# A two-layer decoder trunk: q and k of the attention kept by halves of the sequence, the first pair's groups in that order, and scores ten steps ahead of the values

## The chip, the core and the metric

The kernel runs on one core of a Trainium2 chip. The core's engines have their own instruction queues and run side by side: TensorE (PE) multiplies matrices into PSUM, ScalarE (ACT) and VectorE (DVE) work on PSUM and SBUF, GpSimd (POOL) helps, and SyncE (SP) issues DMA transfers. An instruction that waits holds up everything behind it on its engine. The metric is the device time of one execution in microseconds (us), lower is better.

## The reference

One layer of a gated linear recurrence, one of stick-breaking attention, each followed by a SwiGLU feed-forward network (FFN), all in float32 on a sequence of 1024 tokens with width 1024. The attention, which the change touches, has 16 heads of 64:

```python
qkv = jnp.einsum("bsd,de->bse", x, w_qkv).reshape(bsz, seq, 3, N_HEADS, HEAD_DIM)
...
z = jnp.einsum("bhqd,bhkd->bhqk", qb, kb).astype(jnp.float32) * scale
...
log_fail = jnp.where(strict, jax.nn.log_sigmoid(-z), 0.0)
suffix = lax.cumsum(log_fail, axis=3, reverse=True) - log_fail
weights = jnp.where(strict, jnp.exp(jax.nn.log_sigmoid(z) + suffix), 0.0)
outs.append(jnp.einsum("bhqk,bhkd->bhqd", weights.astype(vb.dtype), vb))
```

Every query attends to earlier keys only; a key's weight is what the later keys left over of the stick.

## The kernel before

**Precision.** PE works on a rounded float32 (`F32R`). A full product is made of three matmuls, hi x hi, hi x lo and lo x hi (`mm3`, L140): each operand is split into a rounded part, copied by ACT, and the rest, subtracted by DVE.

**Pairs, groups and steps.** Heads go in eight pairs `q` of 128 columns. For each pair `qkv_steps(q)` (L1392) computes q, k and v (`which` 0, 1, 2), each for two halves `n` of the sequence (512 tokens). One of these six groups takes eight steps, one `mm3` each, so a pair has 48 steps. Before a `which` begins, the next weights are prepared: `next_weights` (L1377) hands three pieces to the list `later` (ACT copies, DVE subtractions), and `load_link` (L1370) issues on SP a load of weights further ahead.

**What follows a group.** `evacuate` (L1422) scales the product by the normalisation factor `rbc[n]` into `t` (DVE, L1436), and splits it into `two` (ACT L1444, DVE L1445). Four stores on SP then copy q or k into place: q needs hi and lo on different partitions (L1448, L1449), k is wanted twice, in the top and the bottom 64 partitions, for each head of the pair (L1452, `kk<-two`). All four read 64 partitions at a time. The tiles `Q[q][hx]` and `KK[q][hx]` cover all 1024 tokens; half `n` of the sequence fills its columns.

**Scores.** `chunk_list` cuts a head into twelve chunks: eight on the diagonal (row block j = 0..7, 128 to 512 columns of keys of the half j // 4), then four full ones (j = 4..7 against keys of the first half). A chunk is two matmuls on PE (`z_part`, L1481), a sigmoid on ACT and a running product on DVE (`z_rest`, L1493; scans at L1501 and L1504). Chunks 0 to 3 of a head read only the first halves of q and k; chunk 4 is the first that reads the second ones.

**Values.** A head has also twelve units (`unit_list`): `t_part` (L1510) transposes up to four blocks of weights on PE, ACT and DVE split them (`th`, `tl`), and `av_part` (L1530) multiplies them with v.

**The order written out by hand.** The loop at L1627 runs over units u from -LEAD (8) on. In each round PE gets, in this order: the scores of the next chunk, the transposes of unit u + 2, two fill steps (projections of later pairs, from `all_fill`), the values of unit u. ACT and DVE get `th`, `tl`, then the sigmoid and scan of the chunk, then one piece of `later`, then what the fill steps need. So chunk c stands in round c - 8; three extra chunks, in the rounds `gains` (L1621) 31, 29 and 27 from the end, raise the lead to eleven for the last rounds. Pair q's steps fall in the rounds before unit 24q: its first half of k is through in round 24q - 14, its second in 24q - 10.

**The prelude.** Before that loop, 34 steps of pair 0 run alone (L1614): q's two groups, k's two, two steps of v. The normalisation factors aren't known at the start; the dictionary `between` (L1606) places their sums (`stats`), their broadcasts and q's two waiting evacuations between the steps. q's two groups hold their products in the PSUM tiles of the scores (`psZ`), the others use `psQ`.

Of the kernel before, what the change touches and what calls it, by code (L numbers as in the profile page):

```python
# [8 lines left out]
F32 = mybir.dt.float32  # L9
F32R = mybir.dt.float32r  # L10
# [6 lines left out]
P = 128  # L17
S = 1024
D = 1024
ND = D // P  # L20
NT = S // P
NB = 512
NH = S // NB
# [10 lines left out]
def trunk(  # L34
# [22 lines left out]
    nc = tc.nc  # L57
    f32 = lambda t: t.bitcast(F32)
# [40 lines left out]
    xh, xl = [None] * ND, [None] * ND  # L99
# [1230 lines left out]
    NP = HEADS // 2  # L1330
# [12 lines left out]
    with ExitStack() as st:  # L1343
# [33 lines left out]
        def next_weights(raw, lo_eng=nc.vector):  # L1377
            hi, lo = wtile("whi"), wtile("wlo")
            part_hi = lambda i: nc.scalar.copy(half(hi, i), half(raw, i))
            part_lo = lambda i: lo_eng.tensor_sub(half(lo, i), half(raw, i), f32(half(hi, i)))  # L1380

            def second():
                part_lo(0)
                part_hi(1)

            later.extend((lambda: part_hi(0), second, lambda: part_lo(1)))
            k3 = lambda t: t.rearrange("p (k c) -> p k c", k=ND)
            return k3(hi), k3(lo)
# [1 line left out]


        def qkv_steps(q):  # L1392
            for which in range(3):
                w, at = wq.pop((q, which)), 3 * q + which + 1
                if at < 3 * NP:
                    wq[divmod(at, 3)] = next_weights(raws.pop(at))
                else:
                    mix[0].w[mix[0].order[0]] = next_weights(mix[0].raw.pop(0))
                for i in (at + 1,) if at < 3 * NP else (at + 1, at + 2):
                    load_link(i)  # L1400

                ks = (1, 5, 2, 6, 3, 7, 0, 4) if (q, which) == (0, 0) else range(ND)
                for n in range(NH):
                    pool, tag = (psZ, "z") if (q, which) == (0, 0) else (psQ, "qk")
                    ps = pool.tile([P, NB], F32, tag=tag, name="qk_ps")
                    for i, k in enumerate(ks):
                        mm3(ps, w[0][:, k], w[1][:, k], xh[k][n], xl[k][n], i == 0, i == ND - 1)
                        if i == 5 and late:
                            late.pop()()
                        if i < ND - 1:  # L1410
                            yield
                    ev = evacuate(q, which, n, ps)
                    if (q, which) == (0, 0):
                        waiting.append(ev)
                        yield
                    else:
                        next(ev)
                        yield
                        next(ev, None)


        def evacuate(q, which, n, ps):  # L1422
            full = lambda tag, m: [ap.tile([P, m, S], F32R, tag=tag, name=tag, bufs=4) for _ in range(2)]
            t = ap.tile([P, NB], F32, tag="t", name="t", bufs=2)
            cs = slice(n * NB, (n + 1) * NB)
            if which == 2:

                if n == 0:
                    VT[q] = ap.tile([P, S + 1], F32, tag="vt", name="vt", bufs=2)
                    nc.gpsimd.memset(VT[q][:, 0:1], 0.0)  # L1430
                after = VT[q][:, n * NB + 1 : (n + 1) * NB + 1]
                nc.vector.tensor_mul(after, ps, rbc[n])
                yield
                nc.vector.tensor_sub(t, VT[q][:, cs], after)
            else:
                nc.vector.tensor_mul(t, ps, rbc[n])  # L1436
                yield
            if which == 0 and n == 0:
                Q[q] = [t[:, 0] for t in full("q", 1)]
            if which == 1 and n == 0:  # L1440
                KK[q] = full("kk", 2)
            if which < 2:
                two = ap.tile([P, 2, NB], F32R, tag="two", name="two", bufs=2)
                nc.scalar.copy(two[:, 0], t)  # L1444
                nc.vector.tensor_sub(two[:, 1], t, f32(two)[:, 0])  # L1445
                for hx, (a, b) in enumerate(((top, bot), (bot, top))):
                    if which == 0:
                        nc.sync.dma_start(f32(Q[q][hx])[a, cs], f32(two)[a, 0])  # L1448
                        nc.sync.dma_start(f32(Q[q][hx])[b, cs], f32(two)[a, 1])  # L1449
                    else:  # L1450
                        for half_ in (top, bot):
                            nc.sync.dma_start(f32(KK[q][hx])[half_, :, cs], f32(two)[a])  # L1452
                return
            if n == 0:
                VV[q] = ap.tile([P, NT, 2, P], F32R, tag="v", name="v", bufs=2)

            def v_turn():

                pool, tag = (psT, "T") if (q, n) == (NP - 1, 1) else (psQ, "qk")
                tp = pool.tile([P, NB], F32, tag=tag, name="vt_ps")  # L1460
                for i in range(4):
                    nc.tensor.transpose(tp[:, i * P : (i + 1) * P], t[:, i * P : (i + 1) * P], ident)
                src = tp.rearrange("p (b h c) -> p b h c", b=4, h=2)
                bs = slice(4 * n, 4 * n + 4)
                vh, vl = (VV[q][:, bs, :, c] for c in (slice(0, HD), slice(HD, P)))
                nc.scalar.copy(vh, src)
                nc.vector.tensor_sub(vl, src, f32(vh))

            late.append(v_turn)
            if q == NP - 1 and n == 0:  # L1470
                bring_back(*((p, 0) for p in range(NP - 2)))
# [9 lines left out]
        def z_part(q, hx, j, ci, c0, c1, diag):  # L1481
            nk = (j + 1) * P
            ps = psZ.tile([P, NB], F32, tag="z", name="z_ps")
            lhsT = Q[q][hx][:, j * P : (j + 1) * P]
            nc.tensor.matmul(ps[:, 0 : c1 - c0], lhsT=lhsT, rhs=KK[q][hx][:, 0, c0:c1], start=True, stop=False)  # L1485
            nc.tensor.matmul(ps[:, 0 : c1 - c0], lhsT=lhsT, rhs=KK[q][hx][:, 1, c0:c1], start=False, stop=True)  # L1486
            return ps


# [79 lines left out]
        heads = [(q, hx) for q in range(NP) for hx in range(2)]  # L1569
        chunks = [c for q, hx in heads for c in chunk_list(q, hx)]  # L1570
        units = [u for q, hx in heads for u in unit_list(q, hx)]
        LEAD = 8

        def all_fill():
            yield from first
# [25 lines left out]
        with tc.manual_schedule(engines={E.PE, E.Activation, E.DVE, E.Pool, E.SP}):  # L1601


            load_link(1)
            first = qkv_steps(0)
            between = {  # L1606
                12: lambda: stats(rbc[0], psO, "o", 0),
                16: lambda: stats(rbc[1], psO, "o", 1),
                17: lambda: broadcast_r(psO, "o", 0),
                18: lambda: [*waiting[0]],  # L1610
                21: lambda: broadcast_r(psO, "o", 1),
                22: lambda: [*waiting[1]],
            }
            for i in range(1, 2 * ND * NH + 3):  # L1614
                next(first)
                if i in between:
                    between[i]()
                if i > 4 and later:
                    later.pop(0)()

            gains = [len(units) - x for x in (31, 29, 27)]  # L1621

            last_two, out_work = len(units) - 2 * 12, out_fill()
            amount = {x: 2 for x in (-1, 0, 1, 9, 10, 11, 12)}
            amount.update({x: 1 for x in range(14, 21)})
            c = 0
            for u in range(-LEAD, len(units)):  # L1627
                some = chunks[c : c + 1]
                c += 1
                for a in some:  # L1630
                    z = z_part(*a)
                if 0 <= u + 2 < len(units):
                    ready[u + 2] = t_split(t_part(*units[u + 2]), *units[u + 2])
                for a in some:
                    z_rest(z, *a)
                if u - last_two == 1:
                    late.pop()()
                if u - last_two == 9:
                    mix[0].w[mix[0].order[1]] = next_weights(mix[0].raw.pop(1), nc.gpsimd)
                if later:  # L1640
                    later.pop(0)()
                for _ in range(2):
                    next(fill, None)
                for _ in range(amount.get(u - last_two, 0)):
                    next(out_work)
                if u in gains:
                    z_rest(z_part(*chunks[c]), *chunks[c])
                    c += 1
                if u >= 0:
                    av_part(ready.pop(u), *units[u])  # L1650
            while later:
                later.pop(0)()
# [48 lines left out]
```

## Time and profile before

| what | us |
|---|---|
| median of three runs | 2182.03 (2181.58 to 2183.69) |
| the profiled execution | 2182.58 |
| its span, first to last instruction | 2180.8 |
| PE busy in the span | 2165.1 |
| first projection of the attention / first scores / last scores of the last pair start | 956.4 / 986.4 / 1442 |

The profile is of one execution. Busy times are unions of an engine's instructions. Matmul ends are modelled and overlap the next start: two matmuls of 512 columns follow each other every 0.23 us though each is shown with 0.39. In the timeline a row has start, duration, engine, line, operation and tiles, and in brackets the idle time before it with what ended it; in the chain of waits a row has start, duration and what; rows of the waits view have the total, the number of times and the longest; rows of stretches have each engine's busy time with its number of instructions, the granted clock, the DMA share and GB/s. `q` behind an engine's name marks its instruction queue, which issues DMAs.

### The profile page before, as it was taken

What the parts mean: (1) busy time and instruction counts of PE and PEld (TensorE: products, weight loads), DVE (VectorE), ACT (ScalarE), POOL (GpSimd) and SP (SyncE); (2) the same over time, 40 slices, a digit from 0 to 9 for tenths busy, and PEclk for the clock granted to TensorE, in tenths of its full rate; (3) what the DMA queues carried; (4) which work ended last, traced back from release to release, by engine and by line L of the source; (5) the groups of instructions that cost most, each with busy time, mean ns of one, the idle gap of its engine ahead of it and who ended that gap; (6) DMA issues with size and microseconds to landing.
All of it is one profiled execution on the core that took longest, in us unless ns stands there. A gap on an engine that the chain in (4) does not pass through costs nothing.

```text
span 2180.8 us, 27420 instructions
## 1 busy us (share of the span) xinstructions
PE 2165.1 (99%) x10122; PEld 1801.2 (83%) x10122; DVE 1703.7 (78%) x2381; ACT 1077.0 (49%) x1765; POOL 112.2 (5%) x84
## 2 busy tenths in 40 slices
PE   8999999999999999999999999999999999999998
PEld 7888888888888888888888888888888888888887
DVE  7888777767777887887888888886877777788886
ACT  6667445334444544554555555553534444454556
POOL 1222020000000000000000000002000000000002
PEclk9999999999999999999999999999999999999999
DMA  7111412334444764434333344551133444467452
GB/s 233 49 49 39 135 39 73 102 126 157 138 146 139 248 222 129 146 120 101 98 97 93 94 105 107 149 194 55 57 115 119 146 144 149 141 231 233 136 154 87
DMA packets 296101, 277.64 MB, mean 127 GB/s; under 512 B 15256, under 2 KB 210976, under 8 KB 295968
## 3 DMA queue, kind: packets, MB, share of 16 engines
q1 hardware_dynamic: 295808, 275.64, 40.7%
q8 instruction: 79, 1.29, 0.2%
q14 instruction: 54, 0.44, 0.1%
q10 hardware_dynamic: 160, 0.27, 0.0%
HBM read 175.71 MB, written 74.97 MB: 115 GB/s over the span
## 4 chain that ended last, share of the span: by engine, by line
PE 96%; DVE 2%; ACT 1%; DMA 0%; issue 0%; DVEq 0%; SPq 0%; ACTq 0%
PE p_ps L143 18%; PE p_ps L141 18%; PE p_ps L142 18%; PE qk_ps L141 4%; PE qk_ps L143 4%; PE qk_ps L142 4%; PE wt_ps L1515 3%; PE a_ps L142 3%; PE a_ps L143 3%; PE a_ps L141 3%; PE ob_ps L141 3%; PE ob_ps L142 2%; PE ob_ps L143 2%; PE z_ps L1485 2%; PE z_ps L1486 2%; PE av_ps L1537 2%
## 5 line engine op out<-in xcount | busy, mean ns | idle before, releaser
L143 PE MATMUL p_ps<-vh,wbl 128*128 128x512 f32 x524 | 204.2, 390 | 0.2 <-DVE wbl L716 0.2
L143 PE MATMUL p_ps<-vh,wal 128*128 128x512 f32 x524 | 204.1, 389 | 0.1
L141 PE MATMUL p_ps<-vh,wch 128*128 128x512 f32 x524 | 204.2, 390 | 0.0
L141 PE MATMUL p_ps<-vh,wbh 128*128 128x512 f32 x524 | 204.2, 390 | 0.0
L143 PE MATMUL p_ps<-vh,wcl 128*128 128x512 f32 x524 | 204.1, 390 | 0.0
L142 PE MATMUL p_ps<-vl,wbh 128*128 128x512 f32 x524 | 203.9, 389 | 0.0
L141 PE MATMUL p_ps<-vh,wah 128*128 128x512 f32 x524 | 203.9, 389 | 0.0
L142 PE MATMUL p_ps<-vl,wch 128*128 128x512 f32 x524 | 203.9, 389 | 0.0
L142 PE MATMUL p_ps<-vl,wah 128*128 128x512 f32 x524 | 203.8, 389 | 0.0
L1524 ACT CAST th<-wt_ps 128x512 fp32r<-128x512 f32 x192 | 92.1, 480 | 209.6 <-PE wt_ps L1515 209.4
L712 ACT CAST wbh<-sb 128x1024 fp32r<-128x1024 f32 (+2 forms) x69 | 69.6, 1009 | 194.2 <-DVE sb L696 194.2
L1525 DVE TENSOR_TENSOR tl<-wt_ps,th 128x512 fp32r<-128x512 f32 x192 | 106.0, 552 | 62.9 <-ACT th L1524 61.1
L141 PE MATMUL qk_ps<-vh,whi 128*128 128x512 f32 x264 | 118.3, 448 | 0.0
L143 PEld LDWEIGHTS p_ps<-vh,wbl 128*128 128x128 f32 x524 | 98.3, 188 | 22.0 <-DVE wbl L716 1.5
L143 PEld LDWEIGHTS p_ps<-vh,wal 128*128 128x128 f32 x524 | 98.4, 188 | 21.4 <-DVE wal L707 1.0
L143 PEld LDWEIGHTS p_ps<-vh,wcl 128*128 128x128 f32 x524 | 98.3, 188 | 21.2 <-DVE wcl L726 0.7
L142 PEld LDWEIGHTS p_ps<-vl,wah 128*128 128x128 f32 x524 | 98.3, 188 | 20.5
L141 PEld LDWEIGHTS p_ps<-vh,wch 128*128 128x128 f32 x524 | 98.4, 188 | 20.4 <-ACT tb L1103 0.2
L142 PEld LDWEIGHTS p_ps<-vl,wch 128*128 128x128 f32 x524 | 98.4, 188 | 20.4
L142 PEld LDWEIGHTS p_ps<-vl,wbh 128*128 128x128 f32 x524 | 98.4, 188 | 20.4
L141 PEld LDWEIGHTS p_ps<-vh,wbh 128*128 128x128 f32 x524 | 98.4, 188 | 20.3 <-ACT ta L1103 0.2
L141 PEld LDWEIGHTS p_ps<-vh,wah 128*128 128x128 f32 x524 | 98.3, 188 | 20.3
(353 smaller groups left out, 5566.1 us busy)
## 6 DMA issues: line engine op xcount, KB each, us to landing
raw<-in_ffn_w_in SPq DMA_DIRECT2D x88, 512.0 KB, 3.9
vl<-pd SPq DMA_DIRECT2D x128, 256.0 KB, 3.5
pd<-U SPq DMA_DIRECT2D x90, 256.0 KB, 2.3
kk<-two SPq DMA_DIRECT2D x64, 256.0 KB, 3.9
raw<-in_ffn_w_out SPq DMA_DIRECT2D x56, 256.0 KB, 3.7
raw<-in_attn_w_qkv SPq DMA_DIRECT2D x24, 512.0 KB, 4.1
q<-two SPq DMA_DIRECT2D x64, 128.0 KB, 2.3
raw<-in_lru_w_in SPq DMA_DIRECT2D x15, 512.0 KB, 3.9
```

Source lines behind the costliest of these rows:

```text
L141: nc.tensor.matmul(ps, lhsT=wh, rhs=mh, start=first, stop=False, **kw)
L142: nc.tensor.matmul(ps, lhsT=wh, rhs=ml, start=False, stop=False, **kw)
L143: nc.tensor.matmul(ps, lhsT=wl, rhs=mh, start=False, stop=last, **kw)
L712: nc.scalar.copy(self.full(self.wb), self.full(self.sb))
L1485: nc.tensor.matmul(ps[:, 0 : c1 - c0], lhsT=lhsT, rhs=KK[q][hx][:, 0, c0:c1], start=True, stop=False)
L1486: nc.tensor.matmul(ps[:, 0 : c1 - c0], lhsT=lhsT, rhs=KK[q][hx][:, 1, c0:c1], start=False, stop=True)
L1515: nc.tensor.transpose(tp[:, c : c + P], W[q, hx, j, kb // 4][:, (kb % 4) * P : (kb % 4 + 1) * P], ident)
L1524: nc.scalar.copy(th[:, q0:], tp[:, q0:])
L1525: nc.vector.tensor_sub(tl[:, q0:], tp[:, q0:], f32(th)[:, q0:])
L1537: nc.tensor.matmul(ps[:, q0:], lhsT=VV[q][:, kb, hx], rhs=tl[:, q0:], start=False, stop=last)
```

## The change

1. `Q` and `KK` are kept by halves: a tile for each pair, half and head (`Q[q, n][hx]`, `KK[q, n][hx]`) of 512 tokens, eight buffers of half the size in place of four. A store of k now writes rows of two times 512 numbers that lie in one piece. `z_part` picks the half.
2. For pair 0 alone the groups run q half 0, k half 0, q half 1, k half 1, then v. The two first ones wait in `psZ` for their factor; the second evacuation moves from place 22 to 19, ahead of the second broadcast. The next weights and the load ahead come with k's second half for pair 0 (for all other groups with the first half, as before).
3. LEAD is 10. The prelude has 30 steps, `later` is served from step 4 on, and of the three extra chunks only the first is left, so the lead is again eleven from there on.

```diff
         def qkv_steps(q):
-            for which in range(3):
-                w, at = wq.pop((q, which)), 3 * q + which + 1
-                if at < 3 * NP:
-                    wq[divmod(at, 3)] = next_weights(raws.pop(at))
...
+            groups = [(which, n) for which in range(3) for n in range(NH)]
+            if q == 0:
+
+                groups[1:3] = groups[2:0:-1]
+            w = {}
+            for which, n in groups:
+                if which not in w:
+                    w[which] = wq.pop((q, which))
+
+                if n == ((q, which) == (0, 1)):
+                    at = 3 * q + which + 1
+                    if at < 3 * NP:
+                        wq[divmod(at, 3)] = next_weights(raws.pop(at))
...
+                    for i in (at + 1,) if at < 3 * NP else (at + 1, at + 2):
+                        load_link(i)
+                early = q == n == 0 and which < 2
...
+                pool, tag = (psZ, "z") if early else (psQ, "qk")
...
         def evacuate(q, which, n, ps):
-            full = lambda tag, m: [ap.tile([P, m, S], F32R, tag=tag, name=tag, bufs=4) for _ in range(2)]
+            halves = lambda tag, m: [ap.tile([P, m, NB], F32R, tag=tag, name=tag, bufs=8) for _ in range(2)]
...
-            if which == 0 and n == 0:
-                Q[q] = [t[:, 0] for t in full("q", 1)]
-            if which == 1 and n == 0:
-                KK[q] = full("kk", 2)
+            if which == 0:
+                Q[q, n] = [t[:, 0] for t in halves("q", 1)]
+            if which == 1:
+                KK[q, n] = halves("kk", 2)
...
                         for half_ in (top, bot):
-                            nc.sync.dma_start(f32(KK[q][hx])[half_, :, cs], f32(two)[a])
+                            nc.sync.dma_start(f32(KK[q, n][hx])[half_], f32(two)[a])
...
-            lhsT = Q[q][hx][:, j * P : (j + 1) * P]
-            nc.tensor.matmul(ps[:, 0 : c1 - c0], lhsT=lhsT, rhs=KK[q][hx][:, 0, c0:c1], start=True, stop=False)
-            nc.tensor.matmul(ps[:, 0 : c1 - c0], lhsT=lhsT, rhs=KK[q][hx][:, 1, c0:c1], start=False, stop=True)
+            lhsT = Q[q, j // 4][hx][:, j % 4 * P : (j % 4 + 1) * P]
+            for i in range(2):
+                nc.tensor.matmul(
+                    ps[:, 0 : c1 - c0], lhsT=lhsT, rhs=KK[q, ci][hx][:, i, 0 : c1 - c0], start=i == 0, stop=i == 1
+                )
...
-        LEAD = 8
+        LEAD = 10
...
                 18: lambda: [*waiting[0]],
+                19: lambda: [*waiting[1]],
                 21: lambda: broadcast_r(psO, "o", 1),
-                22: lambda: [*waiting[1]],
             }
-            for i in range(1, 2 * ND * NH + 3):
+            for i in range(1, 2 * ND * NH - 1):
                 next(first)
                 if i in between:
                     between[i]()
-                if i > 4 and later:
+                if i > 3 and later:
                     later.pop(0)()
 
-            gains = [len(units) - x for x in (31, 29, 27)]
+            gains = [len(units) - 31]
```

More of the change, by code (lines that the diff above doesn't have):

```diff
@@ L1392, in qkv_steps @@
         def qkv_steps(q):
-            for which in range(3):
-                w, at = wq.pop((q, which)), 3 * q + which + 1
-                if at < 3 * NP:
-                    wq[divmod(at, 3)] = next_weights(raws.pop(at))
-                else:
[L1398 to L1419, printed above, removed]
@@ new lines, in qkv_steps @@
+            groups = [(which, n) for which in range(3) for n in range(NH)]
[9 more added lines that the diff above has]
+                        wq[divmod(at, 3)] = next_weights(raws.pop(at))
+                    else:
+                        mix[0].w[mix[0].order[0]] = next_weights(mix[0].raw.pop(0))
+                    for i in (at + 1,) if at < 3 * NP else (at + 1, at + 2):
+                        load_link(i)
+                early = q == n == 0 and which < 2
+                ks = (1, 5, 2, 6, 3, 7, 0, 4) if (q, which) == (0, 0) else range(ND)
+                pool, tag = (psZ, "z") if early else (psQ, "qk")
+                ps = pool.tile([P, NB], F32, tag=tag, name="qk_ps")
+                wh, wl = w[which]
+                for i, k in enumerate(ks):
+                    mm3(ps, wh[:, k], wl[:, k], xh[k][n], xl[k][n], i == 0, i == ND - 1)
+                    if i == 5 and late:
+                        late.pop()()
+                    if i < ND - 1:
+                        yield
+                ev = evacuate(q, which, n, ps)
+                if early:
+                    waiting.append(ev)
+                    yield
+                else:
+                    next(ev)
+                    yield
+                    next(ev, None)
@@ L1447, in evacuate @@
                     if which == 0:
-                        nc.sync.dma_start(f32(Q[q][hx])[a, cs], f32(two)[a, 0])
-                        nc.sync.dma_start(f32(Q[q][hx])[b, cs], f32(two)[a, 1])
+                        nc.sync.dma_start(f32(Q[q, n][hx])[a], f32(two)[a, 0])
+                        nc.sync.dma_start(f32(Q[q, n][hx])[b], f32(two)[a, 1])
                     else:
                         for half_ in (top, bot):
-                            nc.sync.dma_start(f32(KK[q][hx])[half_, :, cs], f32(two)[a])
+                            nc.sync.dma_start(f32(KK[q, n][hx])[half_], f32(two)[a])
                 return
```

## The prediction

> **What bounds the kernel now.** I read the page first, then the waits of TensorE (PE) in the attention stretch, a table of stretches, and the timeline of one pair of heads engine by engine.
>
> ```profile
> span 2180.8 us, 27420 instructions
> PE 2165.1 (99%) x10122; PEld 1801.2 (83%) x10122; DVE 1703.7 (78%) x2381; ACT 1077.0 (49%) x1765; POOL 112.2 (5%) x84
> ```
> ```profile
> PE wt_ps L1515 <- DVE tl L1525: 1.2, 3, 0.7
> PE z_ps L1485 <- DMA kk<-two: 1.1, 1, 1.1
> ...
> 1183.00:1243.00 60.00, 60.00 (x324) 50.80 (x323) 51.08 (x76) 30.64 (x66) 2.29 (x3) 1.00 0.37 97
> ```
>
> PE is busy 99% of the span. Between 985 and 1470 us only two things hold it: one wait of 1.1 us for the copies of K, and 1.2 us at the very end of attention, where the lead is eleven chunks before and after. A steady stretch (1183 to 1243) has PE busy 60.00 of 60. So ten steps of lead can win at most about 1.1 us, and whatever PE newly waits for is added to the time whole. The question is what the shorter distance to the score matmuls does.
>
> **The one wait that can go (pair 0).** The chain of waits:
>
> ```profile
> 973.54 0.70 DVE t L1436
> ...
> 974.97 0.69 DVE two L1445
> ...
> 979.48 0.70 DVE t L1436
> ...
> 981.62 0.65 SPq L1452
> ...
> 982.31 3.96 DMA kk<-two
> 986.27 0.14 issue
> 986.40 0.35 PE z_ps L1485
> ```
>
> A head's first score matmul needs two of a K half's four stores; they leave SyncE (SP) 0.69 apart, the second lands 3.96 after its issue, and PE goes 0.14 later. Scaling (t) to first store is 2.14 us (979.48 to 981.62). With K's first half computed second, its t can follow q's split, at 974.97 + 0.69 = 975.66, and its first store leaves at 977.80, 3.8 us earlier; the matmul could go at 982.6. The prelude is four steps shorter. Two steps take 1.37 us (1.81 from the transposes at 1215.36 below to the values at 1217.17, less four transposes):
>
> ```profile
> 997.43 0.44 PE wt_ps L1515 x4
> ```
>
> So PE arrives four steps, 2.7 us, sooner. It was ready at about 985.15 (the last projection matmul started at 984.92, and they follow each other every 0.23); now at 982.4. The old loss of 1.25 shrinks to about 0.1: **gain 1.15**.
>
> The moved work issues the same DMAs, in another order: K's first four stores pass q's second four on SP, and the loads of v's and the next q's weights come eight steps later. The split of v's weights then runs on ScalarE (ACT) and VectorE (DVE) behind q's second half (K's first split done at 977.8, then a copy of r, t, copy and subtraction of 0.7 each, and two lo halves of 0.6: 981.8); its first user, step 33, is at about 984.5. K's weights are needed eight steps sooner, at 963.76; their lo halves were written at 961.03 and 962.89 (0.68 each), the second needed only four steps into the group. Both at nothing; without that cover each costs the few tenths by which it is late.
>
> **What comes due two rounds earlier in every pair.** Fill steps keep their place against the transposes and values (34 steps before round -8, as before), so K of pair p is still ready in the same rounds; but chunk 24p is asked for in round 24p-10, not 24p-8, and chunk 24p+4, the first to read K's second half, in 24p-6, not 24p-4. Pair 4, rounds 82 to 90, on PE and SP:
>
> ```profile
> 1206.96 0.39 PE L1536 MATMUL av_ps<-th,v 128*128 128x512 f32 x1
> ...
> 1214.90 0.39 PE L1485 MATMUL z_ps<-kk,q 128*128 128x512 f32 x1
> ...
> 1215.36 0.60 PE L1515 MATMUL wt_ps<-ident,w 128*128 128x128 f32 x4
> ...
> 1217.17 0.28 PE L1536 MATMUL av_ps<-th,v 128*128 128x256 f32 x1
> ...
> 1222.12 0.28 PE L1485 MATMUL z_ps<-kk,q 128*128 128x256 f32 x1
> ...
> 1222.36 0.27 PE L1515 MATMUL wt_ps<-ident,w 128*128 128x128 f32 x1
> ...
> 1224.20 0.34 PE L1485 MATMUL z_ps<-kk,q 128*128 128x384 f32 x1
> ```
> ```profile
> 1211.33 13.29 SPq L1452 DMA_DIRECT2D kk<-two  x8
> ```
>
> K's first half is through PE at 1206.96 (the values follow the fill); its first store leaves at +4.37. Round 86 asks for scores at 1214.90, +7.94: the place chunk 96 moves to. Already in this trace 1211.33 + 0.69 + 3.96 is 1215.98, later than that.
>
> VectorE's order decides the delay:
>
> ```profile
> 1206.99 0.94 DVE L1501 TENSOR_TENSOR_SCAN w<-w,unit 128x384 f32<-128x384 f32 x1
> 1207.85 0.66 DVE L1380 TENSOR_TENSOR wlo<-raw,whi 128x512 fp32r<-128x512 f32 x1
> 1208.44 0.68 DVE L1436 TENSOR_TENSOR t<-qk_ps,rbc 128x512 f32<-128x512 f32 x1
> ...
> 1209.50 1.21 DVE L1501 TENSOR_TENSOR_SCAN w<-w,unit 128x512 f32<-128x512 f32 x1
> 1210.63 0.67 DVE L1445 TENSOR_TENSOR two<-t,two 128x512 fp32r<-128x512 f32 x1
> ...
> 1211.90 1.28 DVE L1504 TENSOR_TENSOR_SCAN w<-w,w 128x512 f32<-128x512 f32 x1
> ```
>
> Both t and the split's subtraction stand behind a round's scan. Two chunks further on, rounds 82 and 83 scan the previous head's full chunks (1.28 each, in place of 0.94 and 1.21): first store at 4.37 + 0.34 + 0.07 = +4.78.
>
> The new transfer has rows of 4 KB in place of 2 KB on both sides; the trace has none like it. Nearest rows:
>
> ```profile
> L1452 SPq DMA_DIRECT2D kk<-two x64: 590/660/1335, 981.6 to 1402.3; - x64
> ...
> DMA to landing us min/median/max: 3.0/3.9/5.4
> ...
> L1449 SPq DMA_DIRECT2D q<-two x32: 461/541/600, 975.7 to 1381.6; - x32
> ...
> pd<-U SPq DMA_DIRECT2D x90, 256.0 KB, 2.3
> ```
>
> I take 0.54 for the first issue (q's stores have the same 64 rows a store) and 3.9 to landing (same source, same 64 partitions, same bytes). Ends: 0.69 for the issue; 2.3 to landing, the row of equal size that runs from all 128 partitions. Beside this, the Trainium skill ("SBUF — State Buffer", section "Door 1: The DMA port swizzle") says partitions 0 to 63 reach only half of the ports and measures 196 GB/s there; an estimate from that is 2.7 us for the two stores' 512 KB whatever the row length, so by that rule the 2.3 end is out and the sum stands; by the other row it would be a gain.
>
> First half: 4.78 + 0.54 + 3.9 + 0.14 = 9.36 against 7.94: **PE waits 1.42**.
>
> Second half, through PE at 1217.17, asked for at 1224.20, +7.03. The rows that delayed it, and those of the narrow chunks that now stand there:
>
> ```profile
> 1217.22 1.28 DVE L1504 TENSOR_TENSOR_SCAN w<-w,w 128x512 f32<-128x512 f32 x1
> 1218.41 0.67 DVE L1436 TENSOR_TENSOR t<-qk_ps,rbc 128x512 f32<-128x512 f32 x1
> ...
> 1220.65 0.67 DVE L1445 TENSOR_TENSOR two<-t,two 128x512 fp32r<-128x512 f32 x1
> ...
> 1221.57 0.42 DVE L1501 TENSOR_TENSOR_SCAN w<-w,unit 128x128 f32<-128x128 f32 x1
> ```
> ```profile
> 1204.41 0.68 DVE L1501 TENSOR_TENSOR_SCAN w<-w,unit 128x256 f32<-128x256 f32 x1
> ```
> ```profile
> 1218.40 0.48 ACT L1524 CAST th<-wt_ps 128x384 fp32r<-128x384 f32 x1 [1.32 <-PE wt_ps L1515]
> 1218.77 0.61 ACT L1498 ACTIVATE w<-z_ps 128x512 f32<-128x512 f32 x1
> 1219.26 0.62 ACT L1444 CAST two<-t 128x512 fp32r<-128x512 f32 x1
> ...
> 1222.88 0.39 ACT L1498 ACTIVATE w<-z_ps 128x256 f32<-128x256 f32 x1
> ```
>
> Now chunk 96 (scan 0.42) and 97 (0.68) are in front: t at +0.47 in place of +1.24. On ACT the copy of th comes 0.22 sooner (scores of 256 columns take 0.24, not 0.46), at +1.01, its sigmoid ends at +1.77, the split's copy at +2.32; DVE scans until +2.48, subtracts until +3.15, first store at +3.2. Landed and seen: 3.2 + 0.54 + 3.9 + 0.14 = 7.78. The scores between change by -0.22, +0.11 and +0.22, so PE arrives at 7.14: **waits 0.64**. Behind the waiting matmul stand the round's transposes and fill, so everything is later by that much.
>
> **Sum.** Pairs 1 to 7: 7 x (1.42 + 0.64) = 14.4. In pair 7 round 161's extra chunk is chunk 172, the first to read K's second half, ahead of that round's values: 0.35 more. Pair 0's second half: PE is at chunk 4 three rounds after chunk 1, at 989.3; K is through at 984.1, its first store leaves at 986.4, seen at 991.0: 1.7. Less the gain: 14.4 + 0.35 + 1.7 - 1.15 = 15.3. The profiled execution took 2182.58 (2180.8 of span and 1.8 around it, untouched), 0.55 above the shown median: 2182.58 + 15.3, **2198 us**.
>
> **Rivals.** (1) *Only the first halves wait*: if the second half's store leaves 0.64 sooner still, 15.3 - 4.5 - 0.35 gives 2193. For it: ACT's and DVE's idle gaps there; against: I already took all of the scan's shortening. (2) *Not slower*: the stores of 4 KB rows land like the 2.3 row, 1.6 sooner. From 1.42 sooner on, no wait of pairs 1 to 7 is left, and pair 0 keeps 0.1: 2182.58 - 1.05 = 2181.5. For it: half the rows per store; against: the minimum of K's 64 stores is 3.0. (3) *The wait is for all four stores of a half*: two more issues of 0.54 and a landing nearer the 5.4 maximum, about 1.9 on each of 15 waits: 2226. Against: in pair 0 the matmul went 0.14 behind the second landing. (4) That the lead isn't ten on PE is excluded by PE keeping the written order in the timeline.
>
> **How the numbers follow.** Forecast 0.66, with a range of its own of 2193 to 2204 (0.15 more for the issue and 0.3 in VectorE's order, on 15 waits); rival 1 0.13; rival 2 0.12; rival 3 0.04; something at the seam to the FFN, either way, 0.05. The range 2188 to 2208 takes in the forecast and rival 1. A measurement here tells about 0.2%, 4.4 us, from no change: rival 2 falls within it. Faster 0.04, same 0.11, slower 0.85.
>
> **What would show it.** PE's waits list the score matmul behind K's stores some 15 times, about 15 to 17 us in all, two per pair, the longer at the chunk that reads K's first half; pair 0's first scores near 982.5; DVE and ACT busy time unchanged; PE no longer 60 of 60. Wrong: stores landing under 3 us, waits of a second kind, or time lost before 980 us.

## The result and the profile after

| | us |
|---|---|
| before, median of six runs beside the changed kernel | 2183.2 (2181.58 to 2183.85) |
| after, median of six runs | 2200.02 (2198.07 to 2200.99) |
| ratio after / before, 95% interval | 1.0078 (1.0068 to 1.0088) |
| the profiled executions, before and after | 2182.58 and 2198.07 |
| their spans | 2180.8 and 2196.3 |

The change makes the kernel slower by 0.8%, or 15.5 us between the two profiled executions. The forecast was 2198.0. That it meets the profiled 2198.07 so closely is in part luck: this execution is the fastest of the six, and the medians lie 16.8 us apart where the forecast had 15.3.

The page of the changed kernel, each engine's busy time, with its share of the span and its number of instructions.

```profile
PE 2167.8 (99%) x10122; PEld 1799.3 (82%) x10122; DVE 1707.2 (78%) x2381; ACT 1077.8 (49%) x1765; POOL 112.4 (5%) x84
```

PE has the same 10122 matmuls and is busy 2.7 us more, DVE 3.5 us more, ACT 0.8 us: the work is the same. The time went into PE standing still. PE's waits in the attention stretch of the changed kernel (970 to 1490 us; total, times, longest):

```profile
PE z_ps L1496 <- DMA kk<-two: 9.5, 11, 1.5
PE z_ps L1496 <- issue: 4.3, 3, 1.6
PE wt_ps L1527 <- DVE tl L1537: 1.2, 3, 0.7
PE z_ps L1496 <- ACT whi L1379: 0.8, 1, 0.8
```

Three of these rows are one thing. They hold 11 + 3 + 1 = 15 waits of a score matmul, 14.6 us in all; wherever the trace has the landing, the wait ends 0.14 us after the second store of a K half has landed, also where the view, which puts a wait down to whatever happened to end last, says "issue" or names a weights copy. Only the 1.2 us at the end of attention stand as before. The steady stretch, in which PE was busy 60.00 of 60 us, shows the same loss:

```profile
1183.00:1243.00 60.00, 58.21 (x310) 48.84 (x310) 49.21 (x73) 29.82 (x65) 2.28 (x3) 1.00 0.36 93
```

The missing 1.79 us are the two waits of pair 4. They stand in the timeline of PE (start, duration, tile sizes; in brackets the idle time before the row):

```profile
1213.78 0.39 PE L1548 MATMUL av_ps<-th,v 128*128 128x512 f32 x1
...
1221.52 0.34 PE L1549 MATMUL av_ps<-tl,v 128*128 128x384 f32 x1
1223.09 0.47 PE L1496 MATMUL z_ps<-kk,q 128*128 128x256 f32 x2 [1.23 <-DMA kk<-two]
...
1225.23 0.28 PE L1548 MATMUL av_ps<-th,v 128*128 128x256 f32 x1
1225.35 0.28 PE L1549 MATMUL av_ps<-tl,v 128*128 128x256 f32 x1
1225.46 0.41 PE L1496 MATMUL z_ps<-kk,q 128*128 128x256 f32 x2
...
1233.08 0.48 PE L1496 MATMUL z_ps<-kk,q 128*128 128x256 f32 x2 [0.56 <-DMA kk<-two]
```

The stores of K's first half, on SP:

```profile
1218.54 3.09 SPq L1462 DMA_DIRECT2D kk<-two  x4
```

The first bracket is the chunk that reads K's first half, the second the one that reads its second half. A score matmul that doesn't wait starts 0.17 before the modelled end of the row ahead of it (1225.46 against 1225.35 + 0.28), so a wait costs about 0.16 us more than its bracket says. The chain of waits of the changed kernel ends each of them in the same way:

```profile
1219.04 3.91 DMA kk<-two
1222.95 0.14 issue
1223.09 0.47 PE z_ps L1496 x2
...
1228.52 0.46 SPq L1462
...
1229.02 3.93 DMA kk<-two
1232.95 0.14 issue
```

The second store goes out 0.50 us after the first (1228.52 and 1229.02), lands 3.9 us later, and PE goes 0.14 after that. What stands ahead of the first store is DVE's and ACT's work; the timeline of pair 4's second half, group through PE at 1225.23:

```profile
1225.27 0.41 DVE L1513 TENSOR_TENSOR_SCAN w<-w,unit 128x128 f32<-128x128 f32 x1
...
1226.89 0.62 ACT L1454 CAST two<-t 128x512 fp32r<-128x512 f32 x1
1227.23 0.68 DVE L1513 TENSOR_TENSOR_SCAN w<-w,unit 128x256 f32<-128x256 f32 x1
1227.82 0.67 DVE L1455 TENSOR_TENSOR two<-t,two 128x512 fp32r<-128x512 f32 x1
...
1228.52 3.09 SPq L1462 DMA_DIRECT2D kk<-two  x4
```

t stands behind the first of these scans and the split's subtraction behind the second, as they stood behind scans before; now they are those of the narrow chunks, 0.41 and 0.68 in place of full ones of 1.28. Pair 0's timeline has the one thing that was won, and its price:

```profile
980.97 0.47 PE L1496 MATMUL z_ps<-kk,q 128*128 128x256 f32 x2
...
986.68 0.62 ACT L1379 CAST whi<-raw 128x512 fp32r<-128x512 f32 x1 [1.34 <-DMA raw<-in_attn_w_qkv]
...
989.57 0.47 PE L1496 MATMUL z_ps<-kk,q 128*128 128x256 f32 x2 [1.55 <-issue]
```

The first scores start at 980.97 without the old wait of 1.1; the chunk that reads K's second half waits 1.55. Start times of the two executions aren't to be compared below some 2 us, because the part of the kernel ahead of the attention differs by that much between executions: here the first projection starts at 954.87, before the change at 956.58. Set back by those 1.7 us, 980.97 fits the 982.5 of the prediction.

### The profile page after: what moved, and what is told of

Same layout as the page of the kernel before. It is cut to its first block, busy times and chain, and to the rows that moved or that the text cites. A ratio compares the mean times of both kernels' runs of the same rounds, so it can differ in the third digit from the quotient of the medians.

```text
span 2196.3 us, 27426 instructions
## 1 busy us (share of the span) xinstructions
PE 2167.8 (99%) x10122; PEld 1799.3 (82%) x10122; DVE 1707.2 (78%) x2381; ACT 1077.8 (49%) x1765; POOL 112.4 (5%) x84
## 3 DMA queue, kind: packets, MB, share of 16 engines
q8 instruction: 79, 1.29, 0.2%
## 4 chain that ended last, share of the span: by engine, by line
PE 91%; DVE 4%; DMA 2%; ACT 1%; issue 1%; SPq 0%; DVEq 0%; ACTq 0%
PE p_ps L143 18%; PE p_ps L141 18%; PE p_ps L142 18%; PE qk_ps L143 3%; PE qk_ps L141 3%; PE qk_ps L142 3%; PE z_ps L1496 3%; PE wt_ps L1527 3%; PE a_ps L142 3%; PE a_ps L143 3%; PE a_ps L141 3%; PE ob_ps L141 2%; PE ob_ps L142 2%; PE ob_ps L143 2%; DMA kk<-two 2%; PE av_ps L1549 1%
## 5 line engine op out<-in xcount | busy, mean ns | idle before, releaser
L1496 PE MATMUL z_ps<-kk,q 128*128 128x512 f32 (+2 forms) x384 | 105.4, 356 | 14.6 <-DMA kk<-two 9.5
```

Source lines behind the costliest of these rows:

```text
L1496: nc.tensor.matmul(ps[:, 0 : c1 - c0], lhsT=lhsT, rhs=KK[q, ci][hx][:, i, 0 : c1 - c0], start=i == 0, stop=i == 1)
```

## The experiments

My theory: the distance alone costs. A lead of ten asks for each half of K two rounds earlier, in 15 places before its second store has landed. Three rivals: the 4 KB rows of the new tiles or the order in pair 0 cost something too; the stores' bytes don't matter; the clock or the moved weight loads have a part in it. Ratios are to the kernel before, measured on the same chip, with 95% intervals.

### Everything of the change but the lead

```diff
-        LEAD = 10
+        LEAD = 8
...
-            for i in range(1, 2 * ND * NH - 1):
+            for i in range(1, 2 * ND * NH + 3):
...
-            gains = [len(units) - 31]
+            gains = [len(units) - x for x in (31, 29, 27)]
```

> Halved tiles and pair 0's new order as in the change, but the lead of 8, its 34 prelude steps and its three extra chunks as before. Theory (the distance from K's stores to the scores costs the time): no PE wait on K's stores is left, pair 0's old wait is gone too; 1.1 us below the kernel before, ratio 0.9995. Rival (the halved tiles with their 4 KB rows, or the new order of pair 0, cost the time): still 10 us or more above, ratio 1.005 to 1.008.

Measured: 2184.95 us, ratio 1.0014 (1.0005 to 1.0022). None of the waits on K's stores is left, as expected, but the kernel is slower, which I hadn't expected. One new wait of PE shows why. The rows are from the waits and the timeline of this kernel, pair 0:

```profile
PE z_ps L1496 <- ACT w L1510: 3.0, 1, 3.0
```
```profile
984.45 0.59 SPq L114 DMA_DIRECT2D raw<-in_attn_w_qkv  x1
...
988.90 1.14 ACT L1379 CAST whi<-raw 128x512 fp32r<-128x512 f32 x2 [3.44 <-DMA raw<-in_attn_w_qkv]
...
991.35 0.55 ACT L1510 ACTIVATE w<-z_ps 128x128 f32<-128x128 f32 x2
```

The load of the next pair's q weights, moved eight steps later and behind q's second stores on SP, went out at 984.5. ScalarE reaches the copy of those weights, stands 3.44 us, and the sigmoids of the first chunks stand behind that copy; PE's next score matmul waits for one of them to read its tile. In the changed kernel the same copy waits 1.34 us (row above), but ACT has done the first chunks' sigmoids by then, and PE doesn't see it.

### The same with the load where it was

The load is issued with pair 0's first group, everything else is the kernel above:

```diff
-                        load_link(i)
+                        if i != 3:
+                            load_link(i)
+                    if at == 1:
+                        load_link(3)
```

> The run with halved tiles and a lead of 8, with one load moved back: that of the next pair's q weights is issued at the first step, not behind q's second stores. Theory (its 3.0 us wait of the scores was ScalarE standing at the copy of weights that hadn't landed, with the sigmoids behind it): that wait goes, no new one comes, 3.0 us less than that run and 1.1 below the kernel before, ratio 0.9995. Rival (the wait comes from the shorter way between the scores and their sigmoids): it stays, ratio 1.0014.

Measured: 2180.68 us, ratio 0.9992 (0.9983 to 1.0001). PE's waits in the attention are the 1.2 us of its end and nothing else:

```profile
PE wt_ps L1530 <- DVE tl L1540: 1.2, 3, 0.7
```

So the 3.0 us were the load's, and the tiles by halves with pair 0's order take away the old wait of 1.1 and bring no other. Whether the kernel is faster for it isn't settled: the median is 1.7 us below, and the interval still holds 1.

### Lead ten, with K two rounds earlier

The changed kernel, with a prelude of 34 steps (so all projections of later pairs come two rounds earlier against the scores) and the early load:

```diff
-            for i in range(1, 2 * ND * NH - 1):
+            for i in range(1, 2 * ND * NH + 3):
```

> The changed kernel, lead 10 and all, but with 34 steps of prelude, so that in every pair K is through PE two rounds earlier against the scores, and with the load of the next pair's q weights at the first step. Theory (only the distance from K's stores to the scores costs): no wait on K's stores in any pair; the fill ends two rounds earlier, which may leave VectorE in front at the end of attention, up to 2.4 us: ratio 0.9995 to 1.0007. Rival (ten steps of lead cost in themselves): still 1.004 or more.

Measured: 2180.82 us, ratio 0.9993 (0.9984 to 1.0002), with no wait on K's stores. Ten steps of lead cost nothing by themselves and bring nothing that these runs can tell from no change. What costs is the distance from K to its first use.

### Lead nine

One round less, with the prelude (32) and the extra chunks (two) to match:

```diff
-        LEAD = 10
+        LEAD = 9
...
-            for i in range(1, 2 * ND * NH - 1):
+            for i in range(1, 2 * ND * NH + 1):
...
-            gains = [len(units) - 31]
+            gains = [len(units) - x for x in (31, 29)]
```

> The changed kernel with a lead of 9, a prelude of 32 steps and two extra chunks. Theory: scores come a round (2.1 to 2.5 us) later against K's stores; the waits of the changed kernel were 1.2 to 1.6 us for the first halves and 0.4 to 0.8 for the second, so none is left in pairs 1 to 7, and pair 0's wait of 1.55 goes too: ratio 0.9995, as with a lead of 8. Rival (each step of lead costs in itself, through ScalarE's and VectorE's order): half of it, about 8 us above before, ratio 1.0035.

Measured: 2182.28 us, ratio 1.0000 (0.9991 to 1.0009). Beside the end's 1.2 us, PE's waits in the attention are two of 0.2: one in pair 0 (at 991.43), and one in pair 7 (at 1403.91), in a round with an extra chunk. My expectation of the next run puts both in pair 0; that is wrong.

The same with the early load:

```diff
-                        load_link(i)
+                        if i != 3:
+                            load_link(i)
+                    if at == 1:
+                        load_link(3)
```

> The changed kernel with a lead of 9 and that early load. Theory: the two waits of 0.2 us that the lead of 9 still showed in pair 0 go as far as they were ScalarE's; 0.2 to 0.4 us under the run with a lead of 9: ratio 0.9993 to 1.0. A difference this small isn't expected to be told from no change; the waits view is to show it.

Measured: 2181.93 us, ratio 0.9997 (0.9988 to 1.0006), one wait of 0.2 in place of two: pair 0's is gone, pair 7's stays (at 1404.56). A round takes PE 2.1 to 2.5 us in pair 4, and the brackets of the pairs behind pair 0 were at most 1.6 with lead ten, so one round covers all but pair 7's 0.2: the loss isn't spread over the two steps of lead, it lies in the second.

### Lead eleven

One round more, prelude of 28 steps, no extra chunks:

```diff
-        LEAD = 10
+        LEAD = 11
...
-            for i in range(1, 2 * ND * NH - 1):
+            for i in range(1, 2 * ND * NH - 3):
...
-            gains = [len(units) - 31]
+            gains = []
```

> The changed kernel with a lead of 11, a prelude of 28 steps and no extra chunk. Theory: every score matmul comes one round (2.3 to 2.5 us) earlier against K's stores; the longer waits become 3.7, the shorter ones about 3.2 with the wider scans that now stand ahead of the split; 7 x 7 and 5 in pair 0, 55 us above before, ratio 1.025. Rival (the waits reached what the scores' order costs and don't grow with the lead): ratio near 1.008.

Measured: 2261.05 us, ratio 1.0366 (1.0345 to 1.0387), 79.8 us more than the kernel before where I expected some 55. The waits come near what was expected:

```profile
PE z_ps L1496 <- DMA kk<-two: 41.9, 13, 3.9
PE z_ps L1496 <- issue: 7.4, 2, 3.8
...
PE z_ps L1496 <- DVE wlo L1380: 1.5, 1, 1.5
```

They come to 50.8 us. The rest is the clock: PE is busy 2193.8 us here, 26.0 more than in the changed kernel, with as many matmuls. The table of stretches shows where (PE, PEld, DVE, ACT and POOL busy, then the granted clock), and the timeline below it the matmuls behind one wait:

```profile
1249.00:1253.00 4.00, 0.47 (x3) 0.43 (x2) 1.11 (x2) 0.00 (x0) 0.00 (x0) 0.76 0.97 220
1253.00:1257.00 4.00, 4.00 (x13) 3.42 (x13) 0.62 (x2) 0.45 (x2) 0.00 (x0) 0.50 0.16 42
```
```profile
1252.60 0.76 PE L1496 MATMUL z_ps<-kk,q 128*128 128x256 f32 x2 [3.53 <-DMA kk<-two]
...
1253.80 0.63 PE L142 MATMUL qk_ps<-vl,whi 128*128 128x512 f32 x1
1254.23 0.63 PE L143 MATMUL qk_ps<-vh,wlo 128*128 128x512 f32 x1
```

After a wait of 3.53 us PE has half its clock for some us: a matmul of 512 columns every 0.43 us, not every 0.23. The records of the clock show 15 such stretches in the attention, 3.4 or 6.8 us long. Against the changed kernel the span is 62.4 us longer (2258.7 and 2196.3): 36.2 more of waiting (50.8 less 14.6) and the 26.0 make 62.2 of it. My expectation had only the waits.

Each of those 15 stretches begins within one of 15 waits, or up to 1.1 us behind it. These waits are 2.88 to 3.87 us long; seven of them have at most 3.02. Length alone doesn't decide it, though: the wait of 3.04 us in the kernel with lead eight and the late load left the clock at full speed. The stretch behind that wait, then the one behind a wait of 3.02 us with lead eleven:

```profile
991.68:995.09 3.41, 3.41 (x15) 2.89 (x16) 3.33 (x6) 1.32 (x3) 0.00 (x0) 1.00 0.94 248
```
```profile
1408.50:1411.50 3.00, 3.00 (x9) 2.52 (x10) 0.62 (x2) 0.95 (x3) 0.00 (x0) 0.50 0.90 234
```

What fits both is where the wait lies. Within a trace the records of half clock begin whole multiples of 3.41 us apart. Counted in such steps, the step ahead of each of the 15 holds at least 2.03 us of waiting (the least from 1247.69 to 1251.10). In the kernel with lead eight a boundary, counted from its own records at 10.87 and 2181.75, falls at 990.50 and parts the 3.04 us into 1.86 and 1.18. No run was made to test this reading.

The Trainium skill ("TensorE: Matmul & The Clock Gate", section "What's actually happening") has PE fall to half its clock after one idle window of about 3.4 us. The steps of 3.41 us agree with such a window, but it needn't be idle as a whole here: waits of 2.88 to 3.02 us, shorter than the window, were enough. The changed kernel, whose longest wait is 1.6 us, has no record of half clock in the attention, and its clock in the stretch from 1183 to 1243 is 1.00.

### The kernel before, with lead ten

Whole-length tiles and the old order of pair 0, and only the lead, the prelude and the extra chunks of the change:

```diff
-        LEAD = 8
+        LEAD = 10
...
-            for i in range(1, 2 * ND * NH + 3):
+            for i in range(1, 2 * ND * NH - 1):
...
-            gains = [len(units) - x for x in (31, 29, 27)]
+            gains = [len(units) - 31]
```

> The kernel before (whole tiles, stores with 2 KB rows, pair 0's old order) with a lead of 10, a prelude of 30 steps and one extra chunk. Theory: the lead alone brings the waits; each is 0.2 us longer than in the changed kernel (stores issued 0.69 apart, not 0.5), and pair 0's first scores wait 4.0 us: 15.5 + 3.9 + 2.8, 22 us above before, ratio 1.010. Rival (halved tiles or 4 KB rows are the cost): only pair 0's 4 us, ratio 1.002.

Measured: 2206.15 us, ratio 1.011 (1.0096 to 1.0123): 23.9 us more than before.

```profile
PE z_ps L1485 <- DMA kk<-two: 17.4, 14, 3.7
PE z_ps L1485 <- issue: 1.8, 1, 1.8
...
PE z_ps L1485 <- ACT whi L1379: 1.0, 1, 1.0
```

20.2 us in 16 waits. The 3.7 is pair 0's old wait of 1.1 with four prelude steps less ahead of it, and behind it the clock was 0.50 for 3.4 us (another 1.7). So with lead ten the tiles by halves and pair 0's order help: the changed kernel has 14.6 us of waits in place of 20.2. They soften what the lead costs, and don't cause it.

### Fewer bytes in the stores

Only k's rounded part is stored, 128 KB a store in place of 256, and both score matmuls read it; the remainder is left out of the scores:

```diff
-                            nc.sync.dma_start(f32(KK[q, n][hx])[half_], f32(two)[a])
+                            nc.sync.dma_start(f32(KK[q, n][hx])[half_, 0], f32(two)[a, 0])
...
-                    ps[:, 0 : c1 - c0], lhsT=lhsT, rhs=KK[q, ci][hx][:, i, 0 : c1 - c0], start=i == 0, stop=i == 1
+                    ps[:, 0 : c1 - c0], lhsT=lhsT, rhs=KK[q, ci][hx][:, 0, 0 : c1 - c0], start=i == 0, stop=i == 1
```

> The changed kernel with stores of k that carry only the rounded part, 128 KB each in place of 256; both score matmuls read it (k's remainder is left out of the scores). Nothing else moves. Theory (the two stores' 512 KB run at about 200 GB/s from 64 partitions and that is what is late): the second landing comes about 1.3 us sooner, the first halves' waits of 1.2 to 1.6 shrink to 0 to 0.3, the second halves' to nothing, pair 0's to 0.3: 1 to 3 us above before, ratio 1.0005 to 1.0015. Rival (a fixed latency of a store decides, not its bytes): ratio stays at 1.0078.

Measured: 2180.36 us, ratio 0.999 (0.9981 to 0.9999), and no wait on K, lower than expected. But this doesn't tell bytes from time: the rounded part is written by ACT ahead of DVE's subtraction, so the stores also left sooner: in pair 4 by 1.58 us for the first half and 0.99 for the second. The next kernel stores the remainder, which is ready only with the subtraction, and leaves the rounded part out of the scores:

```diff
-                            nc.sync.dma_start(f32(KK[q, n][hx])[half_, 0], f32(two)[a, 0])
+                            nc.sync.dma_start(f32(KK[q, n][hx])[half_, 0], f32(two)[a, 1])
```

> As the run with half the bytes, but the stores carry k's remainder, which VectorE writes last, so that they leave as late as in the changed kernel (k's rounded part is left out of the scores). In that run the stores left 1.6 us sooner as well, since ScalarE writes the rounded part first; here only the bytes differ from the changed kernel. Theory (bytes decide): the second store lands about 2.35 us after its issue, not 3.9; the first halves' waits of 1.2 to 1.6 fall to 0 to 0.1, the others to nothing: ratio 0.999 to 1.0005. Rival (the earlier issue did it): landing as late as before, waits stay, ratio 1.007.

Measured: 2182.01 us, ratio 1.0003 (0.9993 to 1.0012).

```profile
PE z_ps L1496 <- issue: 0.5, 1, 0.5
PE z_ps L1496 <- DMA kk<-two: 0.4, 1, 0.4
...
DMA to landing us min/median/max: 2.2/2.3/2.7
```

The same view of the tile in the changed kernel:

```profile
L1462 SPq DMA_DIRECT2D kk<-two x64: 461/606/1285, 976.1 to 1416.3; - x64
...
DMA to landing us min/median/max: 2.9/4.4/4.9
```

The stores leave as late as in the changed kernel (in pair 4 at 4.76 and 3.28 behind the group, there 4.76 and 3.29). Half the bytes land 1.6 us sooner (2.3 against 3.9 for the second store) and PE's waits fall from 14.6 us to 0.9. With 256 KB the four stores of a half land one behind the other: the first 2.9 us after it was issued, the last, issued about 1.8 us later, after 4.9 more; three stores of 256 KB in the 3.8 us between make some 205 GB/s.

The prediction weighed 196 GB/s for 64 partitions from the Trainium skill ("SBUF — State Buffer", section "Door 1: The DMA port swizzle"); the 205 lies 5% above it. The prediction took its estimate of 2.7 us for the two stores' bytes to rule out a landing of 2.3, which it doesn't: counted from the first issue, with the second 0.54 later, it leaves 2.2 behind the second issue.

### K's first half ahead, in every pair

The order q0, k0, q1, k1 for all pairs and not for pair 0 alone; the next weights then come with k's second half in every pair:

```diff
-            if q == 0:
-                groups[1:3] = groups[2:0:-1]
+            groups[1:3] = groups[2:0:-1]
...
-                if n == ((q, which) == (0, 1)):
+                if n == (which == 1):
```

> The changed kernel, lead 10, with the order q half 0, k half 0, q half 1, k half 1 in all pairs (the next weights always come with k's second half, or with the first half of q and v). Theory: K's first half is through PE four rounds earlier, so the seven longer waits of pairs 1 to 7 go (9.0 us, and 0.16 each where the idle time is counted from a matmul's modelled end), the seven shorter ones stay: about 5.5 us above the kernel before, ratio 1.0025, and the waits view lists seven to eight waits on K's stores, about 0.5 us each and 1.5 in pair 0. Rival (the cost isn't the wait for K's first half): stays near 1.0078. If the weights come too late in this order, waits of the projections on DVE or ACT appear.

Measured: 2193.24 us, ratio 1.0048 (1.0035 to 1.0062): less gain than expected. The first halves' waits are gone (pair 4's score matmul starts 0.16 before the modelled end of the row ahead). But the second halves' waits doubled, from about 0.55 to about 1.15. DVE's timeline and the stores, pair 4:

```profile
1223.45 0.67 DVE L1380 TENSOR_TENSOR wlo<-raw,whi 128x512 fp32r<-128x512 f32 x1
1224.03 0.69 DVE L1444 TENSOR_TENSOR t<-qk_ps,rbc 128x512 f32<-128x512 f32 x1
...
1225.70 0.67 DVE L1380 TENSOR_TENSOR wlo<-raw,whi 128x512 fp32r<-128x512 f32 x1
1226.28 0.69 DVE L1453 TENSOR_TENSOR two<-t,two 128x512 fp32r<-128x512 f32 x1
...
1226.99 3.04 SPq L1460 DMA_DIRECT2D kk<-two  x4
```

Two pieces of v's weights (0.67 each) now stand ahead of t and ahead of the split: the first store leaves 4.14 us after the last matmul of the group started, not 3.5. To try that reading, the same kernel with that subtraction on GpSimd, for pairs 1 to 7:

```diff
-                        wq[divmod(at, 3)] = next_weights(raws.pop(at))
+                        wq[divmod(at, 3)] = next_weights(raws.pop(at), nc.gpsimd if q and which == 1 else nc.vector)
```

> The run with the new order in all pairs, with the remainder of v's weights (pairs 1 to 7) subtracted on GpSimd. There the waits for K's second halves were 1.1 to 1.2 us, not 0.5, and the first store left 4.1 us after the group, not 3.5. Theory (v's weights, now due in the same rounds, put two pieces of 0.67 us ahead of the scaling and of the split on VectorE): without them 0.5 to 0.6 a pair again, 4 us less than that run, ratio 1.0028. Rival (without the longer wait ahead of it the second half always starts later): 1.1 us a pair stay, ratio 1.0048.

Measured: 2188.67 us, ratio 1.0035 (1.0022 to 1.0048). The first store again leaves 3.5 us after the group:

```profile
1223.66 0.67 DVE L1453 TENSOR_TENSOR two<-t,two 128x512 fp32r<-128x512 f32 x1
...
1224.35 3.03 SPq L1460 DMA_DIRECT2D kk<-two  x4
```
```profile
1228.95 0.48 PE L1494 MATMUL z_ps<-kk,q 128*128 128x256 f32 x2 [0.60 <-issue]
```

The wait of pair 4's second half is 0.60 again. So it is DVE's order ahead of the split that decides the second halves' wait.

## Why the prediction was right

**What binds, and what a lead can win.** PE had no idle time to fill, so the lead could win only the old wait of 1.1. Shown by the kernel with lead ten and K earlier (0.9993): no K wait, and no time to tell from no change.

**First halves, 1.42 predicted.** The brackets of pairs 1 to 7 are 1.22, 1.56, 1.16, 1.23, 1.51, 1.16 and 1.17, mean 1.29; with the 0.16 that a bracket leaves out, 1.45. The two longest are those of pairs 2 and 5, whose stores landed some 0.2 to 0.3 us later than the other pairs' (the third 4.62 us after its issue, not 4.4); the prediction had one size for all seven. In pair 4 the first store left 4.76 after the values behind the fill (1213.78 to 1218.54; 4.78 predicted), issue, landing and go took 4.55 (4.58), and PE would have been there 7.9 after them (7.94).

**Second halves, 0.64.** Brackets 0.56, 0.52, 0.41, 0.56, 0.56 and 0.63 for pairs 1 to 6, 0.70 with the 0.16. The store left at +3.29 (1225.23 to 1228.52) where 3.2 was predicted. Pair 7's extra chunk: 0.77 + 0.16 = 0.93 against 0.64 + 0.35. Pair 0: 1.55 + 0.16 against 1.7, and its old wait is gone as predicted.

The terms add up to 17.0 for the waits (7 x 1.45 + 6 x 0.70 + 0.93 + 1.71) less about 1.1, 15.9; measured were 15.5 between the profiled executions, 15.3 predicted.

**The price of the transfer.** I took the 3.9 of the old stores over the 2.3 of the row from 128 partitions, because source, partitions and bytes were the same. 3.91 and 3.93 are the chain's. (The first store of a half lands after 2.9, under the 3 that the prediction named as a sign of being wrong; but PE waits for the second.) The runs bear the choice out: twice the length of row with the same bytes left the landing at 3.9, half the bytes brought it to 2.3. What the new tiles brought is the issue: 0.50 between the first two stores in place of 0.63 to 0.69.

**Rivals.** Only the first halves wait: no, the second ones do, 0.41 to 0.77. Stores of 4 KB rows land sooner: no. The wait is for all four stores: no, PE goes 0.14 after the second. All three fell by rows of the changed kernel.

**Moved work "at nothing".** Right for the changed kernel's time, but luckier than the text made it. I priced v's weights' split and the K weights, and said of the next q weights' load only that it comes eight steps later; I didn't name who waits behind it on ACT. With lead eight it costs PE 3.0 us. With lead ten ACT still stands 1.34 us for it, and PE doesn't, because the sigmoids of the first chunks are ahead of the copy.

**What stays open.** Why DVE's busy time is 3.5 us longer was not followed up; the waits aren't the cause, since the kernel with half the bytes, which has none on K, shows 1707.0 too. That a lead of ten costs nothing where K comes earlier was tried together with the early load, not alone. Whether the two versions at 0.9992 and 0.9993 beat the kernel before isn't settled: both intervals hold 1.

## What to carry to other kernels

Before a hand-written order is made to run further ahead, look at the engine that sets the end: if it has no idle time, a longer lead can win nothing, and a producer that isn't moved with it can become a wait. Work out its size as a race between two chains from a common start (here the group's last matmul: evacuation, issue, landing against PE's own rounds), and the slack in rounds tells how many steps of lead are free (here one). A load that moves later can also hold up every instruction behind its first consumer on that engine.

## What was not expected of the hardware

A wait isn't always worth its own length. Waits of up to 1.6 us left PE's clock at 1.00, and so did one of 3.04; 15 waits of 2.88 to 3.87 us with lead eleven, and one of 3.70 with lead ten in the old layout, were followed by 3.4 or 6.8 us at 0.50. With lead eleven 50.8 us of waiting cost another 26.0 us of slow matmuls.
